# Quarters at the end and halves at the start of a six-stage encoder trunk

## The chip, the cores and the metric

The kernel runs on one core of one Trainium2 chip. The metric is the time of one execution on the device, in microseconds; for the kernel before it is the median of three runs. Lower is better.

A core has five engines with queues of their own: PE (TensorE, matmuls; its weight loads are shown as PEld and overlap them), DVE (VectorE), ACT (ScalarE), POOL (GpSimd) and SP (SyncE, which here only issues transfers). Sixteen DMA engines move data between the chip's memory and the on-chip buffers. A queue is worked off in order: an instruction that waits holds up all that stand behind it.

## The reference

Two layers of three residual blocks each, on 256 tokens of width 1024, in float32:

```
for l in range(2):
    x = layer_norm(ALPHA*x + 0.5*swiglu(x, ffn_w_in[l,0], ffn_w_out[l,0]), ln_g[l,0], ln_b[l,0])
    y = mlstm_mixer(x, ...) if l == 0 else window_attention(x, ...)
    x = layer_norm(ALPHA*x + y, ln_g[l,1], ln_b[l,1])
    x = layer_norm(ALPHA*x + 0.5*swiglu(x, ffn_w_in[l,1], ffn_w_out[l,1]), ln_g[l,2], ln_b[l,2])

def swiglu(x, w_in, w_out):          # d_ff = 2816
    gu = x @ w_in
    return (silu(gu[..., :2816]) * gu[..., 2816:]) @ w_out
```

`layer_norm` takes mean and variance over the 1024 columns of a token. The blocks in the middle are a bidirectional mLSTM and a windowed attention; the change does not touch them.

## The kernel before

**Stages.** Six stages follow one another: feed-forward, mLSTM, feed-forward, feed-forward, attention, feed-forward. The tokens are two tiles of 128 (`xt[0]` and `xt[1]`, tokens on the partitions, 1024 columns). Each stage needs x turned over, with the columns on the partitions; that is `xT`, which PE makes by transposes against an identity matrix.

**Three matmuls for one.** Products are made accurate by splitting each operand into a high part (rounded to `fp32r`) and a low part (what is left), and adding hi x hi, hi x lo and lo x hi (`mm3`, three matmuls). So every weight piece that a transfer brings in (`w_raw`, 128 x 1024) is first copied by ACT to `w_hi` (`Weights.high`) and then subtracted by DVE to `w_lo` (`Weights.low`). Likewise every block of `xT` is copied out of its PSUM bank as `xT_hi` and subtracted as `xT_lo` (`split_evac`). The first weight piece is split in two halves of 512 columns (`if i == 0`).

**PSUM.** The eight banks are handed out in two rings of four: `wbank` (named `pw` in the profile) and `ybank` (`py`). A feed-forward stage keeps four `py` banks as its accumulators, `y[t][o]`: token tile t, output half o (512 columns).

**Queues and order.** The order on PE is the order of the program text. Weight pieces are loaded by SP in the order of use, as buffers come free (four to begin with); x comes in four parts of 128 x 512 on ACT's queue. A small planner (`Paced`, `Weights.fill`) decides where in the order the splits of the next weights stand.

**The start** (in `ffn`, `if start`). PE runs 14 filler transposes on the identity (`warm(14)`), then the four transposes of the first part of x, 8 fillers more, and then its first real matmuls (`first_mm`), between which the transposes of the other parts of x stand. The four transposes' bank is evacuated in one piece, the high part by DVE.

**The end** (`tail`, in the last stage). The last six of the 22 chunks of the down projection remain. Tile 0 is finished first. For tile 1 the order is: three chunks of half 1, all six of half 0, and then the last three of half 1:

```
order = [(1, n) for n in range(half)] + [(0, n) for n in range(full)] + [(1, n) for n in range(half, full)]
```

When a half's sum is complete, `Norm.half` adds it to ALPHA times x (a DVE scalar_tensor_tensor) and takes the statistics (bn_stats). `Norm.finish` aggregates them, adds eps, has POOL raise it to the power -0.5, subtracts the mean and multiplies by g in two cuts of 512 columns, and multiplies by the deviation and adds b in two cuts. Each of these last cuts is followed by a transfer to the output, issued by SP. In the profile nearly all instructions have line 138, the helper that records them, so they are told apart by the names of their tiles: `x<-x,py` is the add, `stats<-x` the statistics, `mv<-stats` the aggregate, `x<-x,mv,ln_g` and `x<-x,rs,ln_b` the two scalings, `out_dram<-x` the output.

Of the kernel before, what the change touches and what calls it, by code (L numbers as in the profile page):

```python
# [9 lines left out]
F32 = mybir.dt.float32  # L10
FR = mybir.dt.float32r
AF = mybir.ActivationFunctionType
OP = mybir.AluOpType
# [133 lines left out]
class Weights:  # L147
# [66 lines left out]
    def high(self):  # L214

        nc, i = self.nc, self.made
        p = self.plan[i]
        while self.half and (p["word"] not in self.raw or any(h[0] == p["needs"] for h in self.half)):
            self.low()
        while any(s_[0] == p["needs"] or p["word"] not in self.raw for s_ in self.sums):  # L220
            self.sum()
        if p["word"] not in self.raw:
            return False
        scale, raw = p["scale"], self.raw[p["word"]]
        hi = self.pool.tile([128, D], FR, name="w_hi", tag="w_hi", bufs=RING)
        if i == 0:
            for j in range(2):
                s_ = slice(j * 512, j * 512 + 512)
                nc.scalar.copy(hi[:, s_], raw[:, s_])
        elif scale is None:  # L230
            nc.scalar.copy(hi, raw)
        else:
            nc.scalar.activation(hi, raw, AF.Copy, scale=scale())
        self.half.append((i, hi))
        self.made += 1
        return True

    def low(self):

        nc = self.nc  # L240
        i, hi = self.half.pop(0)
        p = self.plan[i]
        k, scale, raw = p["k"], p["scale"], self.raw[p["word"]]
        lo = self.pool.tile([128, D], FR, name="w_lo", tag="w_lo", bufs=RING)
        if i == 0:
# [75 lines left out]
def trunk_kernel(ctx: ExitStack, tc: tile.TileContext, x, ffn_w_in, ffn_w_out, ln_g, ln_b, ml_w_in, ml_gate_b,  # L321
# [28 lines left out]
    def wide(w, r0, c0):  # L350
        piece(two(w, r0, c0), 2)
# [37 lines left out]
    for j, (kind, l, i, _) in enumerate(stages):  # L389
        if kind == "ffn":  # L390
            wi, wo = ffn_w_in[l, i], ffn_w_out[l, i]
            nth = iter(range(2 * UNITS))

            def down(n):
                for _ in range(n):
                    rows(wo, next(nth))

            for c0 in (0, F):
                for a in range(4):
                    wide(wi, a * 256, c0)  # L400
            for g in range(GROUPS):
                c0 = 512 + 768 * g
                for a in range(4):
                    beside(wi, a * 256, c0, F + c0)
                down(2)
                seven(wi, c0 + 256, F + c0 + 256, lambda i_: down(1) if g < GROUPS - 1 or i_ < 2 else None)
            down(6)
        elif kind == "mlstm":
            for c0 in (1024, 1536):
                for a in range(4):  # L410
                    wide(ml_w_in[0], a * 256, c0)
            for c0 in range(0, 1024, 256):
                for a in range(2):
                    narrow(ml_w_in[0], a * 512, c0)
            for c0 in (2048, 2560):
                for a in range(4):
                    wide(ml_w_in[0], a * 256, c0)
            for c in range(8):
                rows(ml_w_out[0], c, (lambda c=c: gcol[:, c:c + 1]))
        else:  # L420
            for c0 in (1024, 0):
                for a in range(4):
                    wide(at_w_in[0], a * 256, c0)
            for c0 in (512, 768):
# [103 lines left out]
    class Norm:  # L528
        def __init__(self, t, ca, eps, gb, last=False):
            self.t, self.ca, self.eps, self.gb, self.last = t, ca, eps, gb, last  # L530
            self.stats = state.tile([128, 2, 6], F32, name="stats", tag="stats", bufs=2)

        def half(self, h, y):
            z = xt[self.t][:, h * 512:(h + 1) * 512]
            nc.vector.scalar_tensor_tensor(z, z, self.ca, y, op0=OP.mult, op1=OP.add)
            nc.vector.bn_stats(self.stats[:, h], z)

        def finish(self, spare):
            mv = state.tile([128, 2], F32, name="mv", tag="mv", bufs=2)
            nc.vector.bn_aggr(mv, self.stats)  # L540
            rs = state.tile([128, 2], F32, name="rs", tag="rs", bufs=2)
            nc.vector.tensor_scalar(rs[:, 0:1], mv[:, 1:2], self.eps, None, op0=OP.add)
            nc.gpsimd.tensor_tensor(rs[:, 1:2], rs[:, 0:1], mhalf[:, 0:1], op=OP.pow)
# [4 lines left out]
                                               op0=OP.subtract, op1=OP.mult)  # L548
            if len(cuts) == 1:
                W.done(0, spare)  # L550
            for s_ in cuts:
                nc.vector.scalar_tensor_tensor(z[:, s_], z[:, s_], rs[:, 1:2], self.gb[1][:, s_],
                                               op0=OP.mult, op1=OP.add)
                if self.last:
                    nc.sync.dma_start(out[0, tok(self.t), s_], z[:, s_])
            if len(cuts) > 1:
                W.done(0, spare)

    def tail(y, h, todo, first, norm, last, turn_at, between=None):

        def one(t, o, n):
            c, (i, w) = todo[t][n]
            mm3(y[t][o], h(c, t), pair(w, A, 0, slice(o * 512, o * 512 + 512)), first and n == 0, n == len(todo[t]) - 1)

        for o in range(2):
            for n in range(len(todo[0])):
# [9 lines left out]
        for j, (o, n) in enumerate(order):  # L576
            if j == full + turn_at:
                emit_x(0, last)
            one(1, o, n)
            if j >= half and (n < half) == (o == 0):  # L580
                W.done(todo[1][n][1][0] + 1, next(more))
            if n == full - 1:
                norm[1].half(o, y[1][o])
        norm[1].finish(1)
        W.done(most=TD[bound[0]])
        return lambda: emit_x(1, last)
# [5 lines left out]
    def ffn(l, i, n, pending, last):  # L592
        with ExitStack() as ph:
# [10 lines left out]
            start = pending is None  # L604
            if start:
                warm(14)
                to_xT(0, xt[0], ybank, (0,), nc.vector.tensor_copy)
                W.split(1)
                warm(8)
            hs, pieces = [], []  # L610

            def tr(hB, t, h):
# [15 lines left out]

            def first_mm(ps, a):

                def mm(t, i, j):
                    for k in (2 * a, 2 * a + 1):
# [4 lines left out]
                    for t in range(2):  # L637
                        to_xT(t, xt[t], ybank, (1,))
                pieces.extend(W.take(1))
                mm(0, 0, 0)  # L640
                if a == 0:
                    to_xT(1, xt[1], ybank, (0,))
                    W.split(2)
                mm(0, 1, 0)
                if a == 0:
                    mm(0, 0, 1)
                mm(1, 0, 0)
# [763 lines left out]
```

## Time and profile before

| | |
|---|---|
| median of 3 runs | 927.92 us (927.56 to 928.36) |
| the profiled execution | 928.32 us |
| its span, first to last instruction | 926.6 us |
| mean granted TensorE clock | 0.997 |
| PE busy | 916.5 us (99%), 4506 matmuls and transposes |
| DVE, ACT, POOL busy | 785.4 us (85%), 544.4 us (59%), 98.1 us (11%) |
| read from and written to the chip's memory | 185.68 MB, 1.05 MB |

Times within the profile are microseconds from the span's start. In a line of the timeline the first number is when a group starts, the second how long it lasts, then the engine, the line of the kernel, the operation, output<-inputs, the shape and the count; in brackets stands the idle time before it and what ended it. In a line of groups the numbers behind the bar are the busy time in all and the mean of one in ns.

### The profile page before, as it was taken

The page shows a single profiled execution, that of the slowest core. Times are in us where ns is not written, and L with a number is a line of the kernel's source. Part 1 is how long each engine was busy: PE and PEld are TensorE (multiplying, and loading weights), DVE is VectorE, ACT ScalarE, POOL GpSimd, SP SyncE. Part 2 cuts the span into 40 slices and gives each one's busy share as a digit, 9 for nine tenths or more (in the row PEclk, how much of TensorE's full clock was granted, in tenths as well). Part 3 has the DMA queues.
Part 4 walks back from the last instruction along what each step waited for, and adds up shares of the span by engine and source line. Part 5 has one row for each costly group of instructions (what it writes and reads, how often), then busy time and mean ns, then how long its engine had stood idle before and what let it go on. Part 6 is the DMA issues. An engine that isn't in the chain of part 4 may idle for free.

```text
span 926.6 us, 12512 instructions
## 1 busy us (share of the span) xinstructions
PE 916.5 (99%) x4506; PEld 767.3 (83%) x4506; DVE 785.4 (85%) x948; ACT 544.4 (59%) x766; POOL 98.1 (11%) x144
## 2 busy tenths in 40 slices
PE   9999999999999999999999999999999999999996
PEld 7888888889988888888888888888888888888885
DVE  5899997886699799988887899988868878998875
ACT  5656756347664548565636566565569555757460
POOL 0010103011111010101010101010435300110100
PEclk9999999999999999999999999999999999999998
DMA  8979774646535949685558597737434385969421
GB/s 280 356 180 334 216 246 74 229 133 199 188 108 188 344 112 345 166 304 137 160 176 323 144 330 210 269 69 227 156 122 133 101 273 195 274 194 346 122 86 45
DMA packets 98461, 187.54 MB, mean 202 GB/s; under 512 B 6720, under 2 KB 37456, under 8 KB 98400
## 3 DMA queue, kind: packets, MB, share of 16 engines
q1 hardware_dynamic: 91072, 173.04, 54.7%
q0 software_dynamic: 6752, 12.66, 8.6%
q10 hardware_dynamic: 576, 1.05, 0.3%
q8 instruction: 35, 0.57, 0.2%
q14 instruction: 26, 0.21, 0.1%
HBM read 185.68 MB, written 1.05 MB: 202 GB/s over the span
## 4 chain that ended last, share of the span: by engine, by line
PE 87%; DVE 8%; ACT 2%; issue 2%; DMA 1%; POOL 0%; SPq 0%; DVEq 0%; ACTq 0%; POOLq 0%
PE pw L138 56%; PE py L138 30%; DVE w_lo L138 3%; DMA s_raw<-in_ffn_w_in_dram 1%; DVE x L138 1%; ACT w_hi L138 1%; DVE s_raw L138 1%; DVE h L138 1%; DVE stats L138 0%; DVE wt L138 0%; ACT h L138 0%; DVE a_lo L138 0%; DVE hst L138 0%; DVE e L138 0%; DVE S L138 0%
## 5 line engine op out<-in xcount | busy, mean ns | idle before, releaser
L138 DVE TENSOR_TENSOR w_lo<-w_raw,w_hi 128x1024 fp32r<-128x1024 f32 (+1 forms) x237 | 281.8, 1219 | 24.7 <-ACT w_hi L138 22.4
L138 ACT CAST w_hi<-w_raw 128x1024 fp32r<-128x1024 f32 (+1 forms) x237 | 241.7, 1050 | 81.7 <-PE py L138 27.1
L138 PE MATMUL pw<-w_hi,xT_hi 128*128 128x512 f32 x560 | 221.6, 397 | 0.0
L138 PE MATMUL pw<-w_hi,xT_lo 128*128 128x512 f32 x560 | 218.0, 390 | 0.0
L138 PE MATMUL pw<-w_lo,xT_hi 128*128 128x512 f32 x560 | 217.4, 390 | 0.0
L138 ACT CAST w_hi<-s_raw 128x1024 fp32r<-128x1024 f32 x144 | 148.1, 1052 | 80.6 <-DVE s_raw L138 44.0
L138 DVE TENSOR_TENSOR w_lo<-s_raw,w_hi 128x1024 fp32r<-128x1024 f32 x144 | 173.0, 1220 | 22.4 <-ACT w_hi L138 21.9
L138 PE MATMUL py<-w_hi,h_hi 128*128 128x512 f32 x352 | 138.0, 392 | 0.0
L138 PE MATMUL py<-w_lo,h_hi 128*128 128x512 f32 x352 | 137.1, 390 | 0.0
L138 PE MATMUL py<-w_hi,h_lo 128*128 128x512 f32 x352 | 137.1, 390 | 0.0
L138 PEld LDWEIGHTS pw<-w_hi,xT_lo 128*128 128x128 f32 x560 | 105.0, 188 | 22.4
L138 PEld LDWEIGHTS pw<-w_lo,xT_hi 128*128 128x128 f32 x560 | 105.3, 188 | 21.0 <-DVE w_lo L138 0.4
L138 PEld LDWEIGHTS pw<-w_hi,xT_hi 128*128 128x128 f32 x560 | 105.0, 188 | 20.2 <-ACT xT_hi L138 0.2
L138 DVE TENSOR_TENSOR s_raw<-s_raw 128x1024 f32<-128x1024 f32 x72 | 87.2, 1221 | 1.0
L267 POOL DMA_DIRECT2D s_raw<-in_ffn_w_in_dram x24 | 29.2, 1215 | 511.8 <-DVE w_lo L138 469.4
L138 PEld LDWEIGHTS py<-w_hi,h_lo 128*128 128x128 f32 x352 | 66.1, 188 | 13.9
L138 PEld LDWEIGHTS py<-w_lo,h_hi 128*128 128x128 f32 x352 | 66.1, 188 | 13.8 <-DVE w_lo L138 0.3
L138 PEld LDWEIGHTS py<-w_hi,h_hi 128*128 128x128 f32 x352 | 66.1, 188 | 13.5
L138 PE MATMUL pw<-w_hi,S_hi 128*128 128x512 f32 x192 | 74.7, 389 | 0.0
L138 PE MATMUL pw<-w_lo,S_hi 128*128 128x512 f32 x192 | 74.7, 389 | 0.0
L138 PE MATMUL pw<-w_hi,S_lo 128*128 128x512 f32 x192 | 74.7, 389 | 0.0
L138 DVE TENSOR_TENSOR h_lo<-pw,h_hi 128x512 fp32r<-128x512 f32 x44 | 30.2, 688 | 24.4 <-ACT h_hi L138 24.3
(206 smaller groups left out, 1087.6 us busy)
## 6 DMA issues: line engine op xcount, KB each, us to landing
w_raw<-in_ffn_w_out_dram SPq DMA_DIRECT2D x88, 512.0 KB, 5.2
s_raw<-in_ffn_w_in_dram SPq DMA_DIRECT2D x72, 512.0 KB, 6.2
w_raw<-in_ffn_w_in_dram SPq DMA_DIRECT2D x56, 512.0 KB, 5.2
w_raw<-in_ffn_w_in_dram SPq DMA_DIRECT2D x96, 256.0 KB, 4.2
s_raw<-in_ffn_w_in_dram POOLq DMA_DIRECT2D x24, 512.0 KB, 6.0
w_raw<-in_ml_w_in_dram SPq DMA_DIRECT2D x24, 512.0 KB, 4.6
w_raw<-in_at_w_in_dram SPq DMA_DIRECT2D x12, 512.0 KB, 4.7
w_raw<-in_ml_w_out_dram SPq DMA_DIRECT2D x8, 512.0 KB, 4.0
```

Source lines behind the costliest of these rows:

```text
L138: r = f(out, *args, **kw)
L267: nc.gpsimd.dma_start(t.rearrange("p (k f) -> p k f", k=self.words[w]["k"]), v, accum_op=OP.add)
```

## The change

It has two places.

**At the end of the last stage.** The three early chunks of tile 1's half 1 close their group in `y[1][1]`, and their sum is added to ALPHA times x at once (`Norm.first`). The last three chunks are computed by quarters of 256 columns: nine matmuls into one fresh `pw` bank, then nine into another. After each quarter `Norm.quarter` adds its bank to x and takes the statistics of its 256 columns. So three groups of statistics are aggregated instead of two. The last scaling goes by cuts of 512, 256 and 256 columns, and the last of the three output transfers of tile 1 is issued by ACT instead of SP. The statistics tile is made 128 bytes a partition, of which 72 are used; the text of the change says that addresses stay the same modulo 128.

**At the start of the first stage.** The first weight piece is loaded by two transfers, one for each 512 columns, and the second piece too is split by halves (`i < 2`). Of x's first part, the first two blocks are transposed into a `pw` bank of their own and evacuated by DVE alone; then all four are transposed into a `py` bank, of which blocks 2 and 3 are evacuated later (and which serves the later sums as before). There are 6 fillers behind instead of 8. In `first_mm` the matmuls go block by block: one on the first block before the transposes of tile 1, the others after.

```diff
-        if i == 0:
+        if i < 2:                       # in high() and in low()
...
-                    wide(wi, a * 256, c0)
+                    if j == c0 == a == 0:
+                        piece([two(wi, 0, 0)[:, k:k + 1] for k in range(2)], 2)
+                    else:
+                        wide(wi, a * 256, c0)
...
-            self.stats = state.tile([128, 2, 6], F32, name="stats", tag="stats", bufs=2)
+            self.stats = state.tile([128, 32], F32, name="stats", tag="stats", bufs=2)[:, 0:18].rearrange("p (h s) -> p h s", h=3)
+            self.parts = 2
...
+        def first(self, h, y):
+            z = xt[self.t][:, h * 512:(h + 1) * 512]
+            nc.vector.scalar_tensor_tensor(z, z, self.ca, y, op0=OP.mult, op1=OP.add)
+
+        def quarter(self, h, q, y):
+            z = xt[self.t][:, h * 512 + q * 256:h * 512 + (q + 1) * 256]
+            nc.vector.tensor_add(z, z, y)
+            nc.vector.bn_stats(self.stats[:, h + q], z)
+            self.parts = 3
...
-            nc.vector.bn_aggr(mv, self.stats)
+            nc.vector.bn_aggr(mv, self.stats[:, 0:self.parts])
...
-            for s_ in cuts:
+            if self.parts == 3:
+                cuts = [slice(0, 512), slice(512, 768), slice(768, D)]
+            for n_, s_ in enumerate(cuts):
                 nc.vector.scalar_tensor_tensor(z[:, s_], z[:, s_], rs[:, 1:2], self.gb[1][:, s_],
                                                op0=OP.mult, op1=OP.add)
                 if self.last:
-                    nc.sync.dma_start(out[0, tok(self.t), s_], z[:, s_])
+                    (nc.scalar if n_ == 2 else nc.sync).dma_start(out[0, tok(self.t), s_], z[:, s_])
...
+            end = n == len(todo[t]) - 1 or last and t == o == 1 and n == len(todo[t]) // 2 - 1
...
+            if last and j == full + half:
+                break
             one(1, o, n)
+            if last and j == half - 1:
+                norm[1].first(1, y[1][1])
...
+        if last:
+            for q in range(2):
+                yq = wbank((128, 256))
+                for n in range(half, full):
+                    c, (i, w) = todo[1][n]
+                    mm3(yq, h(c, 1), pair(w, A, 0, slice(512 + 256 * q, 768 + 256 * q)), n == half, n == full - 1)
+                norm[1].quarter(1, q, yq)
...
                 warm(14)
-                to_xT(0, xt[0], ybank, (0,), nc.vector.tensor_copy)
+                early = wbank((128, 2, 128))
+                for k in range(2):
+                    nc.tensor.transpose(early[:, k], xt[0][:, tok(k)], ident)
+                split_evac(pair(xT, A, slice(0, 2), tok(0)), early, high=nc.vector.tensor_copy)
+                late = ybank((128, 4, 128))
+                for k in range(4):
+                    nc.tensor.transpose(late[:, k], xt[0][:, tok(k)], ident)
+                turned[0, 0] = late
                 W.split(1)
-                warm(8)
+                split_evac(pair(xT, A, slice(2, 4), tok(0)), late[:, 2:4])
+                warm(6)
...
-                mm(0, 0, 0)
                 if a == 0:
+                    mm(0, 0, 0, (0,))
                     to_xT(1, xt[1], ybank, (0,))
                     W.split(2)
-                mm(0, 1, 0)
+                    mm(0, 1, 0, (0,))
+                    mm(0, 0, 0, (1,))
+                    mm(0, 1, 0, (1,))
+                else:
+                    mm(0, 0, 0)
+                    mm(0, 1, 0)
```

More of the change, by code (lines that the diff above doesn't have):

```diff
@@ L244, in low @@
         lo = self.pool.tile([128, D], FR, name="w_lo", tag="w_lo", bufs=RING)
-        if i == 0:
+        if i < 2:
             for j in range(2):
@@ L562, in one @@
             c, (i, w) = todo[t][n]
-            mm3(y[t][o], h(c, t), pair(w, A, 0, slice(o * 512, o * 512 + 512)), first and n == 0, n == len(todo[t]) - 1)
+            end = n == len(todo[t]) - 1 or last and t == o == 1 and n == len(todo[t]) // 2 - 1
+            mm3(y[t][o], h(c, t), pair(w, A, 0, slice(o * 512, o * 512 + 512)), first and n == 0, end)
         for o in range(2):
@@ L629, in first_mm, with mm @@
             def first_mm(ps, a):
-                def mm(t, i, j):
-                    for k in (2 * a, 2 * a + 1):
+                def mm(t, i, j, ks=(2 * a, 2 * a + 1)):
+                    for k in ks:
                         nc.tensor.matmul(ps[t], xT[i][:, k, tok(t)], pieces[a][j][:, k % 2], start=i == j == k == 0,
```

## The prediction

> **What bounds the kernel now.** I read the chain that ended last on the page first: 87% of it is PE's work. Then the busy time by stretches of the span, because a share over the whole says nothing about the two ends, and the change touches only the ends.
>
> ```profile
> span 926.6 us, 12512 instructions
> ...
> PE 87%; DVE 8%; ACT 2%; issue 2%; DMA 1%; POOL 0%; SPq 0%; DVEq 0%; ACTq 0%; POOLq 0%
> ```
> ```profile
> 1.40:6.90 5.50, 5.45 (x26) 5.35 (x27) 1.28 (x2) 2.42 (x3) 0.00 (x0) 1.00 0.86 295
> 6.90:14.00 7.10, 7.10 (x39) 5.75 (x37) 5.60 (x8) 4.68 (x7) 0.00 (x0) 1.00 0.97 340
> 14.00:900.00 886.00, 884.81 (x4357) 740.75 (x4357) 763.96 (x915) 535.62 (x754) 95.75 (x136) 1.00 0.65 206
> 919.10:926.60 7.50, 0.00 (x0) 0.00 (x0) 4.39 (x8) 0.00 (x0) 0.92 (x1) 0.67 0.18 70
> ```
>
> The first column after each window is its length, the next PE's busy time. From 14 to 900 us PE works 884.8 of 886.0 us: the middle is PE's own work. The changed program has the same instructions in the same order on all five engines there, so nothing in the middle can pay or cost more than the 1.2 us of idle time in it. What is left is 1.45 us before PE's first instruction, the first few microseconds of PE's work, and the 7.5 us from PE's last matmul to the end, in which DVE and the output transfers are alone. The change is an edit of those two ends, and the profile caps it at little more than 1 us of 927.
>
> **The end, step by step.** These are the last DVE instructions, PE's last five matmuls, and the idle gaps in brackets.
>
> ```profile
> 917.79 0.39 PE L138 MATMUL py<-w_lo,h_hi 128*128 128x512 f32 x1
> ...
> 918.70 0.39 PE L138 MATMUL py<-w_hi,h_lo 128*128 128x512 f32 x1
> ```
> ```profile
> 917.09 0.69 DVE L138 SCALAR_TENSOR_TENSOR x<-x,py 128x512 f32<-128x512 f32 x1 [1.65 <-PE py L138]
> 917.81 0.69 DVE L138 BATCH_NORM_STATS2 stats<-x 128x6 f32<-128x512 f32 x1
> 919.12 0.69 DVE L138 SCALAR_TENSOR_TENSOR x<-x,py 128x512 f32<-128x512 f32 x1 [0.62 <-PE py L138]
> 919.85 0.69 DVE L138 BATCH_NORM_STATS2 stats<-x 128x6 f32<-128x512 f32 x1
> 920.58 0.21 DVE L138 BATCH_NORM_AGGREGATE mv<-stats 128x2 f32<-128x12 f32 x1
> ...
> 922.21 1.41 DVE L138 SCALAR_TENSOR_TENSOR x<-x,rs,ln_b 128x512 f32<-128x512 f32 x2
> ```
>
> Between the last matmul's start and DVE's first dependent step lie 919.12 - 918.70 = 0.42 us. Then add, statistics, aggregate, and so on, each waiting for the one before. The change replaces the last nine 512-wide matmuls by eighteen 256-wide ones in two banks, and DVE's one add and one statistics by two of each, half as wide. The nearest rows of those shapes, from the mixers:
>
> ```profile
> 212.68 0.28 PE L138 MATMUL pw<-xT_lo,w_hi 128*128 128x256 f32 x1
> ...
> 213.98 0.28 PE L138 MATMUL pw<-xT_hi,w_hi 128*128 128x256 f32 x1
> ```
> ```profile
> L138 DVE TENSOR_TENSOR wt<-pw,wt 128x256 f32<-128x256 f32 x4 | 1.7, 416 | 0.0
> L138 DVE BATCH_NORM_STATS2 hst<-h 128x6 f32<-128x256 f32 x8 | 3.0, 416 | 0.0
> L138 DVE SCALAR_TENSOR_TENSOR h<-py,den,h 128x256 f32<-128x256 f32 x8 | 3.5, 480 | 2.4 <-ACT h L138 2.4
> ```
>
> *PE.* From the row at 212.68 to that at 213.98 there are eleven steps: 1.30 / 11 = 0.118 us each. At 512 wide, four steps take 918.70 - 917.79 = 0.91, so 0.227 each. The last nine began eight steps before 918.70, at 916.88. Eighteen narrow ones then start their last at 916.88 + 17 x 0.118 = 918.89, 0.19 later than before; but a narrow one is 0.39 - 0.28 = 0.11 shorter, so its result is there 0.31 after its start, at 919.20. The first quarter's is there at 916.88 + 8 x 0.118 + 0.31 = 918.13.
>
> *DVE.* It is busy with the other half until 917.81 + 0.69 = 918.50. First quarter: add and statistics, 2 x 0.416 and two hand-overs of 0.03, to 919.39. That is past 919.20, so DVE and not PE now starts the second quarter: another 0.89, to 920.28. The aggregate starts at 920.31 instead of 920.58: **0.27 us earlier**. The sums after it are unchanged (18 numbers aggregated for 12 is nothing beside its 0.21).
>
> *The early add.* The first three chunks' sum is folded into x ahead of time, one 0.69 us instruction. It stands in DVE's queue before the add at 917.09, which follows 1.65 us of idle time, and its matmuls are over by then (they come first in that tile's order): hidden. Without that cover it would push DVE's whole end by 0.69 and turn the 0.27 into a loss of 0.4.
>
> *The last scaling and the output.* The last two 512-wide steps (1.41 together; one lasts 0.74 by the row below, so they start 0.67 apart) become one of 512 and two of 256. A narrow one lasts 0.48 and, with the same overlap of 0.07, follows 0.41 behind the one before: last end 921.94 + 0.67 + 0.41 + 0.48 = 923.50, against 922.21 + 1.41 = 923.62 before. So the extra cut gives back half of the gain, and 0.12 is left for the last issue. What it buys is a last transfer of 128 KB instead of 256 KB:
>
> ```profile
> 922.88 0.74 DVE L138 SCALAR_TENSOR_TENSOR x<-x,rs,ln_b 128x512 f32<-128x512 f32 x1
> 922.98 0.99 SPq L555 DMA_DIRECT2D out_dram<-x  x2
> ```
> ```profile
> 923.60:924.40 0.80, 0.00 (x0) 0.00 (x0) 0.02 (x1) 0.00 (x0) 0.00 (x0) 0.50 0.72 269
> 924.40:925.40 1.00, 0.00 (x0) 0.00 (x0) 0.00 (x0) 0.00 (x0) 0.00 (x0) 0.50 0.81 309
> ```
>
> The last two columns are the DMA engines' share and GB/s. The two transfers' 524 KB (0.80 x 269 + 1.00 x 309 = 524) flow without a pause to 925.4: the engines are the limit, not the last issue. So what counts is when the first piece starts, and that is 0.27 earlier. By the last issue alone it would be 0.12 plus half a piece, 131 KB at 309 GB/s = 0.42, together 0.54. The smaller of the two holds: that is -0.27. Unknown is how the engines do with rows of 1 KB, which this trace does not write: if a 1 KB row cost as much as a 2 KB row, the two narrow pieces would take 2 x 0.42 longer and the end would be 0.57 later. The added issue on ACT's queue finds it empty: in the window from 919.10 ACT's busy time is 0.00. Ends: -0.54 and +0.57; I take -0.27, since the rate of 309 GB/s is that of 16 engines together, and bytes set it.
>
> [...]
>
> **The start.** Below are PE's, DVE's and ACT's first instructions on data.
>
> ```profile
> 1.45 3.25 PE L138 MATMUL py<-ident 128*128 128x128 f32 x14 [1.45 <-DVE ident L138]
> 4.49 1.06 PE L138 MATMUL py<-ident,x 128*128 128x128 f32 x4
> 5.34 1.81 PE L138 MATMUL py<-ident 128*128 128x128 f32 x8
> 6.91 0.71 PE L138 MATMUL pw<-w_hi,xT_hi 128*128 128x512 f32 x2
> ...
> 10.22 1.03 PE L138 MATMUL py<-ident,x 128*128 128x128 f32 x8
> ...
> 12.92 1.07 PE L138 MATMUL pw<-w_lo,xT_hi 128*128 128x512 f32 x4
> ```
> ```profile
> 5.34 1.14 ACT L138 CAST w_hi<-w_raw 128x512 fp32r<-128x512 f32 x2 [1.03 <-DMA w_raw<-in_ffn_w_in_dram]
> 5.59 0.69 DVE L138 CAST xT_hi<-py 128x512 fp32r<-128x512 f32 x1 [4.19 <-PE py L138]
> ...
> 9.65 1.22 DVE L138 TENSOR_TENSOR w_lo<-w_raw,w_hi 128x1024 fp32r<-128x1024 f32 x1 [0.26 <-ACT w_hi L138]
> ```
>
> Before, the first real matmul's inputs are ready at 5.59 + 0.69 = 6.28 (x) and, for the second one, 5.34 + 1.14 = 6.48 (weights); it starts at 6.91, when the eight filler transposes are through. So the fillers bind. The change halves x's first evacuation and the first weights' load. Two transposes instead of four end 0.43 earlier, at 5.16, and a copy of half the width (0.42, as the narrow DVE rows) ends at 5.58; half the weights are through by 5.34 + 0.57 = 5.91 even if they land no earlier. But PE's queue holds 14 + 2 + 4 + 6 = 26 transposes in front of that matmul, where it held 14 + 4 + 8 = 26. At 0.2 us each (the eight fill 5.34 to 6.91) it still starts at about 6.9. Behind it stand the same twelve matmuls and four transposes up to 10.22, only swapped, in a stretch where PE has no idle time (7.10 of 7.10). Value: 0. Ends: -0.4 (the weights' 6.48 no longer binds a run whose fillers are quicker), +0.1 (one more hand-over).
>
> What is moved there: the second weight piece in halves costs DVE about 0.1 more, behind 9.65, hidden: its low part is done at 10.87 and PE first wants it at 12.92. The first piece's load is two issues on SP's queue, so the next three pieces are issued later, and the changed program makes the fourth piece's load wait for x's first part, which PE transposes from 4.49; all of them stand in transfers that keep the engines full (DMA share 0.86 up to 6.9 and 0.97 up to 14), so an issue some 2 us later costs nothing while earlier pieces are still moving.
>
> **Sum.** 0 at the start and -0.27 at the end: -0.3. The profiled execution took 928.32 us (its span of 926.6 and 1.7 around it), 0.4 above the median of the three, so the changed kernel would take 928.0 in such an execution and 927.92 - 0.3 = **927.6 us** at the median. A measurement of this kernel can tell about 0.2%, 1.9 us, from no change: the forecast is below that.
>
> **Rivals.** *The start pays too (chance 0.2).* If PE's transposes run at the quick rate sooner, the fillers end before 6.28 and the data binds: before, the weights' 6.48; after, about 6.0. Then 0.4 more is gained: 927.2. For it: eight transposes take 1.03 us from 10.22 but 1.81 from 5.34, though the granted clock column says 1.00 in both windows, so when the rate changes decides how long the fillers last. Against it: in this execution it changed only at their end. [...]
>
> *PE stays slow for longer (0.05), the slower side.* [...]
>
> *The end gives nothing (0.15).* Rows of 1 KB or a second queue slow the output by 0.3 to 0.8: 927.9 to 928.4. That the change does not do what it says is excluded by the order of the program's instructions.
>
> **Numbers.** The forecast keeps 0.6. The range takes in the paying start below (927.2 less 0.5, as runs of the kernel before spread over 0.8) and the slow output above: 926.7 to 928.4. For faster than 926.06 no row offers enough: 0.07, for what the rows don't show. Slower than 929.78 would need the slow PE and a slow output together: 0.05.
>
> **What would show it.** Right: the first 512-wide matmul at 6.9 in an execution with the same slow phase; the aggregate 1.1 us after the last matmul's result instead of 1.45; the second quarter's add started by DVE's own queue, not by PE; the transfers' end 0.3 nearer to PE's last matmul. Wrong: narrow matmuls above 0.13 us apart, an idle DVE ahead of the second quarter, an output that lasts as long as before, or a first real matmul well before 6.9 with the rate unchanged.

## The result: slower by 1.0%, and the loss lies in the middle

| | before | after |
|---|---|---|
| median | 928.14 us (927.56 to 928.40, 4 runs) | 937.82 us (937.64 to 938.21, 4 runs) |
| ratio | | 1.0104, 95% interval 1.0089 to 1.0119 |
| profiled execution | 928.32 us, span 926.6 | 937.98 us, span 936.3 |
| mean granted clock | 0.997 | 0.998 |

The forecast was 927.6. The loss of 9.7 us is not at the ends, where the change is, and the clock is the same. These are the page's span and chain for the kernel after, and then its busy time by stretches: length, then busy time and instruction count of PE, PE's weight loads, DVE, ACT and POOL, then the granted clock, the DMA share and GB/s.

```profile
span 936.3 us, 12541 instructions
...
PE 97%; DVE 2%; DMA 0%; ACT 0%; issue 0%; DVEq 0%; ACTq 0%
```
```profile
1.40:6.90 5.50, 5.05 (x23) 4.66 (x24) 1.04 (x3) 2.75 (x4) 0.00 (x0) 1.00 0.85 290
6.90:14.00 7.10, 7.10 (x41) 6.06 (x40) 5.47 (x9) 4.79 (x9) 0.00 (x0) 1.00 1.02 365
14.00:900.00 886.00, 885.14 (x4320) 734.74 (x4319) 756.75 (x908) 528.89 (x749) 96.21 (x136) 1.00 0.65 206
```

From 14 to 900 us PE is as busy as before (885.14 us of 886, before 884.81) at the same granted clock of 1.00, but gets through 4320 matmuls and transposes where it got through 4357. So no wait was added: the instructions themselves come further apart. Which ones, the view of a single tile tells. Its columns are the count, the duration in ns as min/median/max, and first and last start. For one of the three matmuls of each kind, the kernel before:

```profile
L138 PE MATMUL pw<-w_lo,xT_hi x560: 387/389/500, 8.4 to 901.2; 128*128 128x512 f32 x187
L138 PE MATMUL py<-w_lo,h_hi x352: 387/389/504, 42.5 to 918.5; 128*128 128x512 f32 x176
L138 PE MATMUL pw<-w_lo,S_hi x192: 389/389/389, 56.6 to 898.5; 128*128 128x512 f32 x192
L138 PE MATMUL py<-w_lo,q_hi x32: 387/393/404, 699.1 to 740.5; 128*128 128x512 f32 x32
```

and the kernel after:

```profile
L138 PE MATMUL pw<-w_lo,xT_hi x560: 387/389/499, 8.6 to 910.4; 128*128 128x512 f32 x187
L138 PE MATMUL py<-w_lo,h_hi x349: 390/393/497, 42.7 to 925.9; 128*128 128x512 f32 x175
L138 PE MATMUL pw<-w_lo,S_hi x192: 390/393/404, 57.0 to 907.6; 128*128 128x512 f32 x192
L138 PE MATMUL py<-w_lo,q_hi x32: 387/389/395, 706.8 to 747.9; 128*128 128x512 f32 x32
```

The second name is the stationary operand of the kernel's call, the first, w, the moving one; in the trace each such matmul has a weight load beside it, 128x128 where the matmul is 128x512 (`w_lo,S_hi` in the kernel before: 188 ns at the median, and 389). `h` is the gated hidden block, `S` are sums of blocks of `xT` that the feed-forward stages use beside it, `q` is a stationary operand of the attention stage. On xT the median stayed. On h and S the median rose from 389 to 393 ns. On q it fell from 393 to 389: before, q was the slow one. All 192 matmuls on S had taken exactly 389 ns; now none takes less than 390.

Start to start, which is what counts when PE never idles, it is this (mean ns from a matmul's start to the next one's, worked out from all records of the trace):

| 512-wide matmul | count after | before | after |
|---|---|---|---|
| w_hi,h_hi / w_lo,h_hi / w_hi,h_lo | 349 each | 230.1 / 227.5 / 228.9 | 236.2 / 232.5 / 232.0 |
| w_hi,S_hi / w_lo,S_hi / w_hi,S_lo | 192 each | 226.7 / 226.8 / 226.4 | 232.1 / 232.9 / 233.2 |
| w_hi,q_hi / w_lo,q_hi / w_hi,q_lo | 32 each | 249.7 / 232.0 / 233.5 | 247.9 / 227.2 / 229.3 |
| w_hi,xT_hi / w_hi,xT_lo / w_lo,xT_hi | 560 each | 235.0 / 228.4 / 227.5 | 235.9 / 229.4 / 227.7 |

h costs 349 x (6.1 + 5.0 + 3.1) = 5.0 us more, S 192 x (5.4 + 6.1 + 6.8) = 3.5, q 32 x (1.8 + 4.8 + 4.2) = 0.3 less, xT 560 x (0.9 + 1.0 + 0.2) = 1.2 more: 9.4 of the 9.7 us. In the timeline one can count it by hand: 26 steps from the first to the last of these rows, 6.03 us, 0.232 each, where the rows of before gave 0.227.

```profile
920.12 0.40 PE L138 MATMUL py<-w_hi,h_hi 128*128 128x512 f32 x1
920.35 0.39 PE L138 MATMUL py<-w_lo,h_hi 128*128 128x512 f32 x1
920.58 0.39 PE L138 MATMUL py<-w_hi,h_lo 128*128 128x512 f32 x1
...
926.15 0.40 PE L138 MATMUL py<-w_hi,h_lo 128*128 128x512 f32 x1
```

What do h, S and q share that xT does not? Their place. The two statistics buffers were 48 bytes each, in slots of 64: 128 bytes a partition. The changed tile is 128 bytes, two of them 256. Everything that is laid out behind them moves up by 128 bytes: `h_hi` from 141664 to 141792, all S tiles, and the whole of the mixers, `q` with them. What lies ahead stays: the weights, and `xT_hi` at 125024. The table gives places modulo 256, and the distance from the weights to the stationary operand:

| modulo 256 | w | xT | h, S | q | distance xT | h, S | q |
|---|---|---|---|---|---|---|---|
| before | 96 | 96 | 96 | 224 | 0 | 0 | 128 |
| after | 96 | 96 | 224 | 96 | 0 | 128 | 0 |

Every slow kind has distance 128, every quick kind 0. That is only a pattern, and the experiments were made to try it.

At the end of the kernel after, these are the last DVE instructions, PE's first and last narrow matmul, and the output issues:

```profile
926.59 0.69 DVE L138 SCALAR_TENSOR_TENSOR x<-x,py 128x512 f32<-128x512 f32 x1 [1.18 <-PE py L138]
927.31 0.69 DVE L138 BATCH_NORM_STATS2 stats<-x 128x6 f32<-128x512 f32 x1
927.92 0.40 DVE L138 TENSOR_TENSOR x<-x,pw 128x256 f32<-128x256 f32 x1
928.35 0.43 DVE L138 BATCH_NORM_STATS2 stats<-x 128x6 f32<-128x256 f32 x1
928.75 0.42 DVE L138 TENSOR_TENSOR x<-x,pw 128x256 f32<-128x256 f32 x1
929.21 0.43 DVE L138 BATCH_NORM_STATS2 stats<-x 128x6 f32<-128x256 f32 x1
929.67 0.24 DVE L138 BATCH_NORM_AGGREGATE mv<-stats 128x2 f32<-128x18 f32 x1
...
931.33 1.53 DVE L138 SCALAR_TENSOR_TENSOR x<-x,rs,ln_b 128x512 f32<-128x512 f32 x3
```
```profile
926.38 0.29 PE L138 MATMUL pw<-w_hi,h_hi 128*128 128x256 f32 x1
...
928.43 0.29 PE L138 MATMUL pw<-w_hi,h_lo 128*128 128x256 f32 x1
```
```profile
L138 ACTq DMA_DIRECT2D out_dram<-x x1: 353/353/353, 932.9 to 932.9; - x1
...
DMA to landing us min/median/max: 2.0/2.1/2.1
```

And at the start:

```profile
1.45 3.25 PE L138 MATMUL py<-ident 128*128 128x128 f32 x14 [1.45 <-DVE ident L138]
5.09 0.69 PE L138 MATMUL pw<-ident,x 128*128 128x128 f32 x2 [0.40 <-DMA x<-in_x_dram]
5.58 1.06 PE L138 MATMUL py<-ident,x 128*128 128x128 f32 x4
6.43 0.98 PE L138 MATMUL py<-ident 128*128 128x128 f32 x6
7.17 0.48 PE L138 MATMUL pw<-w_hi,xT_hi 128*128 128x512 f32 x1
```

These two ends are taken up with the prediction's steps below.

### The profile page after: what moved, and what is told of

It reads as the page before. It is cut to its first block, busy times and chain, and to the rows that moved or that the text cites. A ratio compares the mean times of both kernels' runs of the same rounds, so it can differ in the third digit from the quotient of the medians.

```text
span 936.3 us, 12541 instructions
## 1 busy us (share of the span) xinstructions
PE 926.0 (99%) x4515; PEld 769.0 (82%) x4515; DVE 786.7 (84%) x954; ACT 544.1 (58%) x768; POOL 98.5 (11%) x144
## 3 DMA queue, kind: packets, MB, share of 16 engines
q10 hardware_dynamic: 720, 1.18, 0.3%
## 4 chain that ended last, share of the span: by engine, by line
PE 97%; DVE 2%; DMA 0%; ACT 0%; issue 0%; DVEq 0%; ACTq 0%
PE pw L138 63%; PE py L138 34%; DVE w_lo L138 1%; DMA x<-in_x_dram 0%; DVE x L138 0%; DVE h L138 0%; DVE stats L138 0%; ACT w_hi L138 0%; ACT xT_hi L138 0%; ACT h L138 0%; DVE q_lo L138 0%; DVE hst L138 0%; ACT sg L138 0%; ACT q_hi L138 0%; DVEq L1449 0%
```

## The experiments

Times are compared with the kernel before in the same set of runs; its median was 928.79, 929.53 and 929.32 us in the three sets, with single runs from 927.7 to 931.6. So a difference below about 1 us is told by the traces, not by these times.

**1. The changed kernel with one statistics buffer.** One buffer of 128 bytes takes as much room as the two had before. The layout is that of before, all else is the change.

```diff
-... state.tile([128, 32], F32, name="stats", tag="stats", bufs=2)[:, 0:18]...
+... state.tile([128, 32], F32, name="stats", tag="stats", bufs=1)[:, 0:18]...
```

> The changed kernel with one statistics buffer of 128 bytes instead of two, so that every tile of the stages lies where it lay before the change. Theory (place): the loss is the 128 bytes by which all tiles of the stages moved, +5 ns for each 512-wide matmul whose stationary operand lies there; then 927.9 to 928.6 us, and the matmuls on h and S start 0.227 us apart again. Rival (ring): the extra bank at the start turns the ring of pw banks by one, and with it what each matmul collides with; then 937 to 938 us, as the change.

Measured: 928.16 us (927.50 to 928.72, 11 runs), ratio 0.9991 (0.9982 to 1.0000). The loss is gone with one number changed. The tile views:

```profile
L138 PE MATMUL py<-w_lo,h_hi x349: 387/389/497, 42.3 to 916.1; 128*128 128x512 f32 x175
L138 PE MATMUL pw<-w_lo,S_hi x192: 389/389/389, 56.4 to 898.1; 128*128 128x512 f32 x192
L138 PE MATMUL py<-w_lo,q_hi x32: 387/393/404, 699.2 to 740.5; 128*128 128x512 f32 x32
```

h and S are back at 389, q back at 393. So neither the quarters nor the halves cost the 9.7 us.

**2. The kernel before with the large statistics tile, and nothing else.**

```diff
-... state.tile([128, 2, 6], F32, name="stats", tag="stats", bufs=2)
+... state.tile([128, 32], F32, name="stats", tag="stats", bufs=2)[:, 0:12]...
```

> The kernel before with nothing but the statistics tile made 128 bytes a partition (two buffers), so that the tiles of the stages move up by 128 bytes. Theory (place): 937 to 938 us, with 0.232 us between matmuls on h and S. Rival (ring): 928 us, since neither the order nor the banks change.

Measured: 937.94 us (2 runs), ratio 1.0095 (1.0077 to 1.0114), span 936.6.

```profile
L138 PE MATMUL pw<-w_lo,S_hi x192: 389/394/405, 57.7 to 908.1; 128*128 128x512 f32 x192
L138 PE MATMUL py<-w_lo,q_hi x32: 387/390/396, 707.3 to 748.4; 128*128 128x512 f32 x32
```

The enlarged tile alone makes the whole loss, with the order and the banks of before, so it is not the ring either. With the first run this shows what causes it: the size of this buffer. That it acts by where it puts the others is what the next runs try.

**3. The changed kernel with a still larger tile.** Two buffers of 192 bytes: everything behind them moves up by 256 instead of 128.

```diff
-... state.tile([128, 32], F32, name="stats", ...
+... state.tile([128, 48], F32, name="stats", ...
```

> The changed kernel with statistics tiles of 192 bytes, so that the tiles of the stages lie 256 bytes above their place before the change. Theory (place, and it repeats every 256 bytes): 928 to 928.6 us. Rival (any move away from the old place costs, or the period is longer than 256): 937 to 938 us. Ring: 937 to 938 us too.

Measured: 928.21 us (927.51 to 929.62, 10 runs), ratio 0.9994 (0.9985 to 1.0003).

```profile
L138 PE MATMUL pw<-w_lo,S_hi x192: 388/389/390, 56.1 to 898.9; 128*128 128x512 f32 x192
```

More room and a larger shift, and no loss. It is not the amount of memory or the height of the address: a shift of 256 bytes costs nothing (S at 389 ns again).

**4. The changed kernel, weights and xT moved up too.** 128 bytes of unused constants lie ahead of everything: w and xT move by 128, h and S by 256. So h and S stand at 96 modulo 256 again, as before, but the weights no longer do.

```diff
+    pad = consts.tile([128, 32], F32, name="pad")
+    nc.gpsimd.memset(pad[:, 0:1], 0.0)
```

> The changed kernel with 128 bytes more of constants, so that weights and xT move up by 128 bytes and the tiles of the stages by 256 in all. Two forms of the place theory part here. If the stationary operand's own place modulo 256 decides, matmuls on h and S are at 0.227 again and those on xT (1680 of them) become slow at 0.232: about 928.3 + 8 = 936 to 937 us. If it is its place against the moving weights, matmuls on xT stay at 0.227 and those on h and S stay at 0.232: 937 to 938 us, told apart by the spacings in the trace.

Measured: 937.41 us (2 runs), ratio 1.0090 (1.0071 to 1.0108).

```profile
L138 PE MATMUL pw<-w_lo,xT_hi x560: 387/390/505, 7.8 to 909.8; 128*128 128x512 f32 x187
L138 PE MATMUL pw<-w_lo,S_hi x192: 389/394/405, 56.3 to 907.0; 128*128 128x512 f32 x192
```

h and S are in their good old place and still slow (on S 232 to 233 ns start to start); xT has left its place together with the weights and is still quick (median 227). So it is neither the stationary operand's own place nor the weights' own: it is the distance between the two.

**5. Distance 64.** The kernel before with two statistics buffers of 96 bytes.

```diff
-... state.tile([128, 2, 6], F32, name="stats", tag="stats", bufs=2)
+... state.tile([128, 24], F32, name="stats", tag="stats", bufs=2)[:, 0:12]...
```

> The kernel before with statistics tiles of 96 bytes, so that the tiles of the stages lie 64 bytes up. Theory (only the half of 256 matters, one step): either 928 or 937.9 us. Rival (the price grows with the distance): between, about 933 us.

Measured: 939.64 us (2 runs), ratio 1.0111 (1.0092 to 1.0129).

```profile
L138 PE MATMUL pw<-w_lo,S_hi x192: 393/394/398, 58.6 to 909.7; 128*128 128x512 f32 x192
```

A distance of 64 costs at least as much as 128 does: neither nothing nor, as the rival had it, half.

**6. Distance 32.** The kernel before with one statistics buffer of 160 bytes.

```diff
-... state.tile([128, 2, 6], F32, name="stats", tag="stats", bufs=2)
+... state.tile([128, 40], F32, name="stats", tag="stats", bufs=1)[:, 0:12]...
```

> The kernel before with one statistics buffer of 160 bytes, so that the tiles of the stages lie 32 bytes up and nothing else is changed. Theory (stationary and moving operand have to lie on the same place modulo 256): any other distance costs, so 0.232 to 0.234 us between matmuls on h and S and 937 to 940 us. Rival (only distances of 64 and more, or of a whole 64-byte line, cost): 928 to 929.5 us.

Measured: 939.31 us (2 runs), ratio 1.0103 (1.0079 to 1.0128).

```profile
L138 PE MATMUL pw<-w_lo,S_hi x192: 395/396/397, 57.7 to 908.9; 128*128 128x512 f32 x192
```

Distances of 32 and 64 cost as much as 128 or a little more: 232 to 234 ns start to start, nearly every single matmul, where at 128 about one in seven stayed quick (229 ns or less). So the rule is not "the same modulo 128", nor modulo 64 or 32. Of the distances tried, only 0 and 256 are free.

**7. Everything up by 32 together.** The kernel before with 32 bytes of unused constants ahead of all: no distance changes.

```diff
+    pad = consts.tile([128, 8], F32, name="pad")
+    nc.gpsimd.memset(pad[:, 0:1], 0.0)
```

> The kernel before with 32 bytes more of constants, so that weights, xT and the stages' tiles all move up by 32 bytes together: the distance between stationary and moving operand stays 0, but all begin on a multiple of 128. Theory (only the distance counts): 928 to 929.5 us, matmuls on xT, h and S at 0.227. Rival (the operands' own place counts as well): every 512-wide matmul changes, either way, by several us in all.

Measured: 929.93 us (8 runs), ratio 1.0006 (0.9994 to 1.0019), span 926.7.

```profile
L138 PE MATMUL pw<-w_lo,S_hi x192: 388/389/390, 57.1 to 898.6; 128*128 128x512 f32 x192
L138 PE MATMUL py<-w_lo,q_hi x32: 387/393/398, 699.6 to 741.0; 128*128 128x512 f32 x32
```

The same 32 bytes that cost 10 us when the weights stay behind cost nothing when they come along, and q stays as slow as it was.

One more rival can be settled from these traces: that PE collides with what the other engines or the transfers do at that moment in the same buffers. Some steps from one h matmul to the next stand clear of that, with DVE, ACT, POOL and the DMA engines all idle from 0.2 us before to 0.2 us behind. There are 9 in the kernel before, at 226.7 ns on average, 10 in the kernel after, at 231.8, and 10 in experiment 6, at 233.4. So the price does not need the others at work: 5 to 7 ns a step are paid with all of them idle.

**8. The start alone**, on the kernel before. Besides the lines below it has the new order in `first_mm`.

```diff
-        if i == 0:
+        if i < 2:
...
-                    wide(wi, a * 256, c0)
+                    if j == c0 == a == 0:
+                        piece([two(wi, 0, 0)[:, k:k + 1] for k in range(2)], 2)
+                    else:
+                        wide(wi, a * 256, c0)
...
-                to_xT(0, xt[0], ybank, (0,), nc.vector.tensor_copy)
+                early = wbank((128, 2, 128))
...
-                warm(8)
+                split_evac(pair(xT, A, slice(2, 4), tok(0)), late[:, 2:4])
+                warm(6)
```

> The kernel before with the change's start alone (halved first part of x, halved first two weight pieces); all tiles lie as before. Forecast's theory: fillers bind, 0, so within 0.2 us of the kernel before. Rival (x's first part lands later behind one more transfer): the changed kernel's first 512-wide matmul started at 7.17 instead of 6.91 us after a 0.40 us wait of PE for x; then +0.2 to +0.3 us, and the wait is in this trace too.

Measured: 928.68 us (11 runs), ratio 0.9994 (0.9985 to 1.0003). The times can't tell it from nothing. The rival's wait for x is in its trace (0.44 us, and the first 512-wide matmul at 7.48), but such waits come with the old start too. Its profiled execution is used below.

**9. The end alone**, on the kernel before, with one statistics buffer so that nothing moves. `Norm.first`, `Norm.quarter` and the group's early close are as in the change.

```diff
-            self.stats = state.tile([128, 2, 6], F32, name="stats", tag="stats", bufs=2)
+            self.stats = state.tile([128, 32], F32, name="stats", tag="stats", bufs=1)[:, 0:18]...
...
+            if self.parts == 3:
+                cuts = [slice(0, 512), slice(512, 768), slice(768, D)]
...
-                    nc.sync.dma_start(out[0, tok(self.t), s_], z[:, s_])
+                    (nc.scalar if n_ == 2 else nc.sync).dma_start(out[0, tok(self.t), s_], z[:, s_])
...
+                norm[1].quarter(1, q, yq)
```

> The kernel before with the change's end alone (early add, quarters, three cuts of the output), with one statistics buffer so that all tiles lie as before. Forecast's theory: the aggregate 0.27 us nearer to the start of the last nine chunks' matmuls and the end of the span 0.27 nearer, so -0.3 us. Rival (the end gives it back): the aggregate is 0.3 to 0.4 nearer, but the last transfer takes its 2.0 us from issue to landing whatever its size, and what follows its landing is longer; then 0 to +0.2 us.

Measured: 929.07 us (11 runs), ratio 0.9998 (0.9989 to 1.0007). The times can't tell this from nothing either; the trace, which is read below, shows the end 0.2 us shorter.

**10. All distances at 0.** The changed kernel with one statistics buffer, and one of attention's small tiles enlarged by 128 bytes, which moves q to distance 0 (and the stage's other tiles behind it with q).

```diff
-            self.stats = state.tile([128, 32], ..., bufs=2)...
+            self.stats = state.tile([128, 32], ..., bufs=1)...
...
-            minus_one = tile_([128, 16], F32, "minus_one")...
+            minus_one = tile_([128, 48], F32, "minus_one")...
```

> The changed kernel with one statistics buffer, and besides the attention stage's tiles moved up by 128 bytes by a larger first tile of that stage. Theory (place of the stationary operand against the weights): the 96 matmuls of the output projection on q, 0.232 us apart before, go to 0.227: 0.3 to 0.5 us less than the same kernel without that move (928.16), so 927.7 to 927.9. Rival (some other operand of that stage pays for it, such as the scores' matmuls): no less.

Measured: 927.97 us (927.44 to 928.96, 11 runs), ratio 0.9984 (0.9975 to 0.9993). This is the one interval of the twelve that lies below 1, but the two runs that follow, with the same layout, don't repeat it.

```profile
L138 PE MATMUL py<-w_lo,q_hi x32: 387/389/395, 699.7 to 740.7; 128*128 128x512 f32 x32
```

q is cured as predicted by the rule. But the rule pays for only 32 x (1.8 + 4.4 + 4.0) = 0.3 us of the 1.6 by which the medians differ; the rest is within what the runs of this set scatter, and is not explained. The median is just above the 927.7 to 927.9 that were expected.

**11 and 12. Quarters without the third cut.** The kernel of experiment 10 with the output in two cuts of 512 on SP, as before, and the first weight piece in one load; the second of the two also with the start of before.

```diff
-            if self.parts == 3:
-                cuts = [slice(0, 512), slice(512, 768), slice(768, D)]
...
-                    (nc.scalar if n_ == 2 else nc.sync).dma_start(out[0, tok(self.t), s_], z[:, s_])
+                    nc.sync.dma_start(out[0, tok(self.t), s_], z[:, s_])
...
-                    if j == c0 == a == 0:
-                        piece([two(wi, 0, 0)[:, k:k + 1] for k in range(2)], 2)
-                    else:
-                        wide(wi, a * 256, c0)
+                    wide(wi, a * 256, c0)
```

> The changed kernel with one statistics buffer and the attention stage up by 128 bytes (927.97 before), and in addition the output of the last tile in two cuts of 512 on SP's queue, and the first weight piece in one load. Theory (the end gives back its gain: one more DVE cut, and a last transfer whose landing SP looks at first and then has seven more to look at): the time from PE's last matmul to the end falls from 7.8 to about 7.4 us, so 0.3 to 0.4 less: 927.6. Rival (the smaller last transfer does pay): no less than 928.0.

> The same as e11 but with the start of the kernel before. Theory (the start is worth nothing beyond the spread of when x lands): within 0.3 us of e11, 927.5 to 928. Rival (the halved start pays when x lands early): 0.3 to 0.5 us more than e11.

Measured: 929.82 us (12 runs), ratio 1.0000 (0.9990 to 1.0010), and 928.79 us (12 runs), ratio 0.9992 (0.9982 to 1.0003). The first run's time fits its rival (no less than 928.0) and not the 927.6 expected. The second lies 1.0 below the first, which neither of its expectations had. In the profiled executions the end did become shorter, by 0.4 us (below); the times are too scattered to show it.

## Why the prediction was wrong, point by point

**The step that failed** is the one that looked safest: "The changed program has the same instructions in the same order on all five engines there, so nothing in the middle can pay or cost more than the 1.2 us of idle time in it." The order was the same. But idle time bounds only what can be gained by waiting less; what an instruction itself costs was taken as fixed by its shape, and it was not. About 1,600 matmuls became some 5 ns dearer (experiments 1 and 2). No rival had the middle in it, so none came near the time.

Two things at hand spoke against that step. The first was in the profile of before: the same instruction, 512 wide, took 389 ns on xT, h and S and 393 on q (fourth row of the kernel before, above). Two prices for one shape mean that something besides the shape sets the price. The second was in the change: a tile that grows moves its neighbours, and "the same modulo 128" is a claim about a rule that no row of the profile had shown. The runs differ, at one width, one granted clock (1.00 from 14 to 900 us) and one shape: on S 226.4 to 226.8 ns in the kernel before and 232.1 to 233.2 in the kernel after, by where the operands lie.

**The start: 0 was forecast.** The step was right in outcome and partly in its reason. PE's queue does hold the same 26 transposes, and no gain can be seen: the start alone gives 0.9994. But the fillers did not bind alone. PE stood idle for x for 0.40 us, ahead of 5.09 us (the bracket above), because x's first part landed later than in the profile of before (4.49). That is not the change's doing: over the profiled executions of all these kernels, PE's first transposes of x began between 4.49 and 5.43 us with the old start, and between 4.87 and 5.36 with the new one. The first 512-wide matmul began between 6.41 and 7.79 us with the old, and between 6.36 and 7.83 with the new, 7.17 in the one shown. So one execution's start can't tell a part of a microsecond, and the first rival (the start pays) stays neither shown nor excluded at 0.4 us. Its condition did occur: in three executions the transposes had their quick rate (0.11 us each) by the time x was there. From x's first transpose to the fortieth 512-wide matmul it took 12.37 and 12.38 us with the old start (experiments 12 and 9) and 11.89 with the new (experiment 4). That is the rival's gain, but in a single execution with the new start. The second rival, a PE that stays slow for longer, did not come about: with a gap of 0.40 the first real matmul was 0.26 later than before. The chance of more than 929.78 counts on it too, but no run shows that a gap makes PE slow: the first two 512-wide matmuls took 1.20 us together behind a gap of 0.62 (experiment 5), 0.70 behind one of 0.84 (experiment 9), and 0.71 in the kernel before.

**PE and DVE at the end: right, and a little under.** The narrow matmuls came (928.43 - 926.38) / 17 = 0.121 us apart (forecast 0.118; 0.119 in experiment 12, at distance 0, so at this width the distance of 128 went with 0.002 us a step), and the second quarter's add, at 928.75, has no bracket: DVE's own queue started it, as forecast. From the start of the last nine chunks' matmuls to the aggregate it was 920.58 - 916.88 = 3.70 before and is 929.67 - 926.38 = 3.29: 0.41 earlier, where 0.27 was forecast. The term that was mis-sized is the hand-over: the adds start before the statistics ahead of them are through (927.31 + 0.69 = 928.00, add at 927.92), not 0.03 behind. The early add was hidden as forecast: idle time of 1.18 us still follows it.

**The extra cut: as forecast.** From aggregate to last issue it took 923.65 - 920.58 = 3.07 before and 932.90 - 929.67 = 3.23 now: 0.16 of the 0.41 is given back (forecast 0.15).

**The output: wrong.** "So what counts is when the first piece starts" took the transfers as bound by bytes. They were not: the last transfer, 128 KB instead of 256, is among the five of the row above, which took 2.0 to 2.1 us from issue to landing. The view of the output tile in the kernel before, where all are 256 KB:

```profile
L555 SPq DMA_DIRECT2D out_dram<-x x4: 332/335/347, 914.8 to 923.6; - x4
...
DMA to landing us min/median/max: 2.0/2.0/2.1
```

So the smaller last piece bought nothing, and the end followed the last issue.

**And a wait that no step had.** The end of the span is not the last landing. By the trace's semaphore events SP, before it ends, looks at the semaphores of the transfers one after another, in ten steps of about 0.06 us each where it need not wait. In the kernel before, the last transfer's came last: SP got past it at 925.69 and went on at 925.76. In the kernel after it comes third: SP got past it at 934.94, seven more steps of this kind followed, and SP went on at 935.44. That costs 0.43 us more. The start alone shows it, where nothing of the end was changed but one more load at the start shifts the order: from its last matmul at 918.81 to the end of its span (927.12 in the trace) it takes 8.31 us, against 926.58 - 918.70 = 7.88 before, though its aggregate follows as before (920.68 - 918.81 = 1.87; before 1.88).

```profile
span 927.1 us, 12518 instructions
```
```profile
918.81 0.39 PE L138 MATMUL py<-w_hi,h_lo 128*128 128x512 f32 x1
```
```profile
920.68 0.21 DVE L138 BATCH_NORM_AGGREGATE mv<-stats 128x2 f32<-128x12 f32 x1
```

So the end adds up otherwise than forecast: -0.41 for the aggregate, +0.16 for the cut, 0 for the bytes, +0.43 for SP's order, together +0.18. Measured from the start of the last nine chunks, it is 926.58 - 916.88 = 9.70 before and 936.26 - 926.38 = 9.88 after. The forecast had -0.27.

Experiment 9, the end without the additional load, hardly pays for SP's order: its last transfer's semaphore comes last again. These are its span, its first narrow matmul and its aggregate:

```profile
span 927.8 us, 12535 instructions
```
```profile
918.25 0.28 PE L138 MATMUL pw<-w_hi,h_hi 128*128 128x256 f32 x1
```
```profile
921.52 0.24 DVE L138 BATCH_NORM_AGGREGATE mv<-stats 128x2 f32<-128x18 f32 x1
```

The aggregate follows after 3.27 us, and the span (927.76 in the trace) ends 9.51 after the start of the nine chunks: 0.19 less than before. That is near the forecast's 0.27, but by luck: the aggregate gained 0.43, and the third cut with what follows it gave about half of that back, where the forecast had let the bytes of the output decide. Experiment 12, with quarters but the two old cuts and the old loads, keeps the whole 0.41. Its span and first narrow matmul:

```profile
span 927.1 us, 12533 instructions
```
```profile
917.83 0.28 PE L138 MATMUL pw<-w_hi,h_hi 128*128 128x256 f32 x1
```

From there to the end of its span (927.12) it takes 9.29, 0.41 less than before. Experiment 11, which has the new start but no additional load, takes as long as experiment 12. Each of these is one profiled execution; no comparison of times is fine enough to confirm them.

**The sum.** With the layout kept (experiment 1) the change measures 0.9991 (0.9982 to 1.0000); the forecast of 0.3 us less is a ratio of 0.9997. The two ends were too little to measure, as the prediction had said. The 9.7 us came from a line that it had read as bookkeeping.

**What stays open.** Why the matmuls come further apart at the distances 32, 64 and 128 was not found out: the runs show the condition and the price, not the mechanism. At distance 128 the price is paid where only one of two neighbours lies off: from an xT matmul to one on h the step took 226.6 ns before and 232.5 after (32 steps), from h to xT 226.9 and 234.5 (23). The rows on xT, whose distance did not change, rose by 0.2 to 1.0 ns, which is 1.2 of the 9.7 us. Such steps account for some of it. The rest is not scatter: of the w_hi,xT_lo steps 72% to 75% took 229 ns or less in every run with h and S at distance 0, and 56% to 66% in the others. With all other engines idle it did not show (the few such steps from xT to xT took 226.6 to 226.8 ns on average in the two kernels), and its cause stays open. On h and S the distances 0, 32, 64, 128 and 256 were tried; q, moved along with them, stood at 160 in experiment 6 and was slow (w_lo,q_hi 231.6 and w_hi,q_lo 235.5 ns start to start; in the kernel after, at 0, 227.2 and 229.3), and at 192 in experiment 5 and was so in part (229.4 and 232.0). 96 and 224 were not tried.

## What to carry to other kernels

Before calling a stretch untouched because its instructions and their order are the same, compare where its operands lie: a tile that grows moves all that is laid out behind it. Where one shape shows two durations in a profile, find out what sets the price before summing with either; here it is the distance between stationary and moving operand, and keeping it at 0 modulo 256 bytes saved some 5 of 232 ns on each 512-wide matmul concerned. Here that was about 1,600 of 4,500 matmuls and 1% of the kernel. Two ways of letting a tile grow cost nothing here: giving the room back (one buffer instead of two, 928.16 us in experiment 1), and moving what lies behind it by 256 bytes in all (928.21 us in experiment 3).

## What the runs showed of the hardware

- On S, a 512-wide fp32r matmul with its weight load followed the one before after 0.226 to 0.227 us with stationary and moving operand at the same place modulo 256 bytes (kernel before), after 0.232 to 0.233 at a distance of 128 (kernel after), and at 64 and 32 after up to 0.234 (experiments 5 and 6). Moving both together left the medians where they were: 389 ns on S when all moved by 32 (experiment 7), and 0.227 us from start to start on xT when w and xT moved by 128 (experiment 4). With all other engines and the transfers idle, the steps on h took 226.7 ns in the kernel before and 231.8 in the kernel after. At 256 wide it was 0.121 us at distance 128 (kernel after) and 0.119 at 0 (experiment 12).
- In the kernel after, the five output transfers, of 128 KB in rows of 1 KB and of 256 KB in rows of 2 KB, landed 2.0 to 2.1 us after their issue; in the kernel before, the four of 256 KB did so too.
- The order in which SP looked at finished transfers was worth 0.43 us at the end of the kernel after (0.50 us from the last transfer's semaphore until SP went on, 0.07 before), and with one more load at the start alone (experiment 8) the end of the span came 8.31 us behind the last matmul's start, 7.88 before.
